# The forward substitution of 32x32 blocks in a hybrid decoder step: from VectorE to GpSimd, with GpSimd's order pinned

## The chip, the cores and the metric

One core of a Trainium2 chip runs the whole program. The metric is the device time of one execution in microseconds (us), from the profiler's clock of the core; the kernel's time is the median of several runs. The engines are named as the profile names them: PE is TensorE (matmuls; PEld its weight loads), DVE is VectorE, ACT is ScalarE, POOL is GpSimd, SP issues the DMAs.

## What is computed

One layer of a hybrid decoder for 2048 new tokens of one sequence and for 8 running sequences with 4 tokens each; the model's width is 1024, all in float32. The normalised rows are multiplied by one wide input weight; a gated convolution and an RWKV-7 time mixing use the product; two output weights, gates, a last weight and a norm close the layer. What matters here is the time mixing, for each of 16 heads:

```python
def step(S, inp):
    r_t, k_t, v_t, d_t, kk_t, a_t = inp
    sa = jnp.einsum('bhvk,bhk->bhv', S, -kk_t)
    S = (S * d_t[:, :, None, :] + sa[..., None] * (kk_t * a_t)[:, :, None, :]
         + v_t[..., None] * k_t[:, :, None, :])
    y = jnp.einsum('bhvk,bhk->bhv', S, r_t)
    return S, y
```

Done in chunks of 64 tokens, the recurrence needs, for each chunk and head, the inverse of a 64x64 unit lower triangular matrix. The kernel inverts its two 32x32 diagonal blocks by forward substitution and joins them by small matmuls.

## The kernel before

**Tiles and stages.** The 2048 tokens are four sets of 512 (the sample tokens go with the last). The main stream of each set is blocks of 24 matmuls: 8 slices of the contraction, each with three products of rounded parts (high by high, low by high, high by low), 128x128 weights by 512 columns, into one of three PSUM banks (`ip`). Each block's result is evicted by ACT and DVE. In set 0 a weight is loaded raw into `wraw`, split into its high and low parts in `whl` (ACT copies the high part, DVE subtracts: the instruction whl<-wraw,whl) and stored; later sets load the parts back.

**The pairs.** Between the main stream's matmuls runs the time mixing of one pair of heads after the other, 8 pairs in each of 4 sets, 32 in all, as `Side` generators: keys (from the projected k, r, v to the scaled AR, BK), solve, merge (the 32x32 inverses joined into Xbd), load (transposes), chain (the recurrence over 8 chunks: pa, UB, pb, SV, S), out (normalisation of the rows Yc and the store). Each has a part of the pair's share of the main stream, from the table CUTS (line 31): its fourth number is where the keys end and the solve begins, its fifth where the solve ends and merge and load begin.

**The solve** (rwkv_solve, line 1177). PE makes the 64x64 scores of 8 chunks and 2 heads, DVE masks them into GM, ACT copies the diagonal blocks to Mc, DVE transposes these into Mi (2.06 us), and then come 31 steps j = 31 to 1 of two instructions on [128, up to 76]: a product into tt and a sum into X. The last step is a 32x32 transposition of X into a tile that bears the name Mi too (in the profile: Mi<-X). Then ACT copies it into Xbd, DVE transposes a part into Mc (Mc<-Xbd), and PE's first merge matmuls read it (pt<-Mc,GM and pt<-Mc,Mo).

**What sets the order.** PE, ACT, DVE and POOL each take their instructions in order. While the program is written, a `Clock` (line 51) places every instruction at an estimated start, from costs per engine and from the ends of what it reads; a Side goes on when its inputs are ready by that clock. For the engines in PLANNED (line 48: DVE and ACT) the order of these starts is pinned at the end (line 1792), except for the kinds in LOOSE, the low parts of the weights among them. POOL's instructions are placed by the same clock, but not pinned. `held` (line 148) keeps the stretches in which DVE, with two inputs that aren't in PSUM, or POOL would hold up the other.

**On POOL before**: the product cv by the gate in the convolution, the two last instructions of out (tmp<-tmp,bv and tmp<-tmp,sz), the power in the norms (mu_), one-column copies between the token shift's `carry` and the tile q (mixed_block, line 838: tmp<-carry when a k, r, v or z block begins, carry<-tmp when it ends; the eviction of a block reads that column), and every second low part of the next set's rows (XL in to_cols, line 754, called from prep, line 765).

Of the kernel before, what the change touches and what calls it, by code (L numbers as in the profile page):

```python
# [11 lines left out]
ALU = mybir.AluOpType  # L12
AX = mybir.AxisListType
PSUM = bass.MemoryType.PSUM
DRAM = bass.MemoryType.DRAM

P = 128
# [10 lines left out]
     "sv": 1.5, "bt": 2.0, "score": 4.0, "inv0": 5.0, "inv": 0.45, "inv1": 4.0, "merge": 2.0,  # L28
     "gk": 1.3, "us": 1.3, "sa": 1.3, "state": 1.3, "samp": 2.0, "gn": 4.0, "out": 2.0}

CUTS = {"most": (0.7, 0.0, 0.0, 0.34, 0.7, 0.95, 0.95), "last": (0.6, 0.3, 0.68, 0.4, 0.7, 0.97, 0.9),
        "end": (0.2,0.03,0.22,0.1,0.25,0.32,0.28)}

TAIL = (0.32,0.52,0.32,0.52,0.65)
# [10 lines left out]
SLACK = 60.0  # L45


PLANNED = ('DVE', 'ACT')


LOOSE = ('prep', 'first', 'late', 'zero', 'low')
# [3 lines left out]
OVERLAP = {"DVE": (83, 13), "ACT": (60, 18)}  # L55


class Clock:
# [72 lines left out]
    def ready(self, aps):  # L131
        return max([e[4] for ap in aps for e in self._hits(ap)], default=0.0)

    def add(self, eng, outs, ins, cost, lag=60.0):
        start = max([self.t["PE"] - PAST if eng in self.busy else self.t[eng]] + [e[4] for ap in ins for e in self._hits(ap) if e[6] != eng] +
                    [e[4] - 26.0 if eng in OVERLAP else e[5] for ap in (*ins, *outs) for e in self._hits(ap) if e[6] == eng] +
                    [self.touched.get((eng, ap.tensor.name), 0.0) for ap in (*ins, *outs)] +
                    [e[5] + 60.0 * (e[7] != eng) for ap in outs for e in self._hits(ap)])
        took = cost
        if eng in OVERLAP:  # L140
            over, drain = OVERLAP[eng]
            p0 = self.boxes(outs[0])[0][0]
            took = cost - over if p0 == 0 else cost + over + 2 * drain
        if eng in self.busy:
            start = self.gap(eng, start, took)
        if eng == "POOL" or eng == "DVE" and sum(ap.space != PSUM for ap in ins) > 1:
            for _ in range(3):
                was = start
                for s, e in sorted(self.held["POOL" if eng == "DVE" else "DVE"]):
                    if s < start + cost and start < e:  # L150
                        start = e
                start = self.gap(eng, start, took)
                if start == was:
                    break
            self.held[eng] = self.held[eng][-60:] + [(start, start + cost)]
        end = start + cost
        for ap in (*ins, *outs):
            self.touched[eng, ap.tensor.name] = start
# [95 lines left out]
class Traced:  # L254
# [5 lines left out]
    def __getattr__(self, op):  # L260
        f = getattr(self.eng, op)

        def call(*a, **k):
            r = f(*a, **k)  # L264
# [6 lines left out]
            at = self.clock.add(self.name, outs, ins, c, late + 60.0)  # L271
            if self.clock.planning and self.clock.kind not in LOOSE and self.name in PLANNED:
                self.clock.begun.setdefault(self.name, []).append((at, r.ins))
            return r
        return call

    def cost(self, op, out, ins, k):
        n = out.free_size()
        if self.name == "PE":
            turned = op == "transpose"  # L280
            lhs, rhs = (ins[0], ins[1]) if turned else (k["lhsT"], k["rhs"])
            part = [next(x for x in (32, 64, 128) if v <= x) for v in (lhs.ap[0][1], lhs.free_size())]
            mode = tuple(part)
            if turned:
                t, late = max(0.85 * n, 30.0), 272.0
            elif rhs.dtype == F32R:
                mode, t, late = (P, P), 8 + 0.4375 * n, 175 + 0.43 * n
            elif mode == (P, P):
                t, late = max(1.667 * n + 3, 216.0), max(382.0 if n >= P else 328.0, 175 + 1.7 * n)
            elif mode == (32, 32):  # L290
                t, late = 30.5 * max(1.0, n / 32), 212.0
            elif mode[1] == 64:
                t, late = (59.6 if mode[0] == 64 else 55.4) * max(1.0, n / 64), 300.0
            elif mode == (64, P):
                t, late = (0.93 * max(n, 64) if n <= P else 0.93 * n), 250 + 1.7 * n
            else:
                t, late = 1.667 * max(n, 32), 300.0
            if mode != self.clock.mode:
                t, late = t + 165, late + 225
                self.clock.mode = mode  # L300
            return t, late - t + SLACK
        if self.name == "DVE":
            per = {"transpose": 1.12 if n <= 256 else 1.86, "tensor_tensor_scan": 2.1, "reciprocal": 6.1}.get(op, 1.05)
            if op == "tensor_reduce":
                n = ins[0].free_size()
            if op == "tensor_scalar" and ins[0].space != PSUM:
                per = 0.587
            one = op == "scalar_tensor_tensor" and isinstance(k["scalar"], bass.AP)
            return 145 + per * n + 58 * one
        if self.name == "ACT":  # L310
            strided = n > 64 and list(ins[0].ap)[-1][0] > 1
            return (155 if ins[0].space == PSUM else 190) + (1.9 if strided else 0.84) * n + 100 * max(0, len(ins) - 1) + 0.0
        if k.get("op") == ALU.pow:
            return 1650.0
        return 120 + 2.3 * n if op == "tensor_tensor" else 120 + 1.0 * n


class Queue:
# [26 lines left out]
def hybrid_kernel(tc, x_prompt, x_sample, state_conv, state_shift, state_rwkv, norm_g, w_in, conv_w,  # L345
# [6 lines left out]
    SP = Queue(nc.sync, clock)  # L352
# [214 lines left out]
    TPS = NT // P  # L567
# [197 lines left out]
    def prep(th, half):  # L765
# [9 lines left out]
        yield "free", xts  # L775
        for q in range(NB // KG):
            for k, (i, xt) in enumerate(zip(mine, xts)):
                to_cols(q, xt, (i - th * TPS) * P, G if k % 2 else V)
                if q == NB // KG - 1 and i < NTL - 1:
                    wraw_p.free(xt)  # L780
                yield 1
# [14 lines left out]
    def late_setup():  # L796

        for i in range(TPS, NTL + 1):
            xt, m = load_x(i)
            yield 1, [xt[0:m]]  # L800
            stat_tile(i, xt, m)
            if i < NTL:
                wraw_p.free(xt)
            yield 1
# [372 lines left out]
    def rwkv_solve(th, p, o):  # L1177
# [7 lines left out]
        for c0 in range(0, NCH + samp, 4):  # L1185
# [6 lines left out]
            k = len(cs)  # L1192
# [22 lines left out]
        for j in range(31, 0, -1):  # L1215
            c0 = j // 4
            tt = sm.tile([P, 80], F32, name="tt")
            tv = tt[:, 0:(8 - c0) * j].rearrange("p (c i) -> p c i", i=j)
            V.tensor_tensor(out=tv, in0=Mi[:, j, 0:j].unsqueeze(1).broadcast_to([P, 8 - c0, j]),
                            in1=X[:, c0:8, j:j + 1].broadcast_to([P, 8 - c0, j]), op=ALU.mult)  # L1220
            V.tensor_tensor(out=X[:, c0:8, 0:j], in0=X[:, c0:8, 0:j], in1=tv, op=ALU.add)
            yield W["inv"]
        Xo = rw.tile([P, 32, 32], F32, name="Mi")[:, 0:8].rearrange("p a (e c) -> p a e c", c=8)
        V.transpose(Xo.rearrange("p a e c -> p (a e c)"), X.rearrange("p a b -> p (a b)"))
        o.update(GM=GM, Xo=Xo, Mo=Mo)
        yield W["inv"]

    def rwkv_merge(th, p, o):

# [330 lines left out]
    def part_of(w, key, j, src, scale=1.0):  # L1560

        hl = qs[turns[0] % 2]
        turns[0] += 1
        yield 1, [src]
        A.activation(out=hl[:, 0], in_=src, func=AF.Copy, scale=scale)
        yield 1, [hl[:, 0]]
        V.scalar_tensor_tensor(out=hl[:, 1], in0=src, scalar=scale, in1=hl[:, 0].bitcast(F32), op0=ALU.mult, op1=ALU.subtract)
        SP.store(units[w][key][j // 2][:, :, j % 2 * 4 * P:(j % 2 + 1) * 4 * P], hl.bitcast(F32))
# [561 lines left out]
```

## Time and profile before

| | |
|---|---|
| median of 3 runs | 3086.65 us (3082.61 to 3088.28) |
| profiled execution | 3081.61 us; its span, first to last instruction, 3079.9 us |
| granted TensorE clock, mean | 0.995 |
| busy: PE, DVE, ACT, POOL | 3004.7, 2140.3, 1338.9, 311.2 us |

A line of instructions reads: line in the code, engine, operation, output<-inputs, partitions x columns, count | busy us, mean ns of one | idle time of the engine ahead of them and who ended it. Nearly all stand under line 264, the helper that records each call, so one goes by the tiles. A line of waits reads: who waited <- for whom: us in total, times, the longest. A line of the timeline reads: start, duration in us, engine, operation, count [idle before <- who ended it]. In a line of windows stand the busy time and the count of PE, PEld, DVE, ACT and POOL. Times in a timeline and a window count from the span's start.

### The profile page before, as it was taken

The page shows a single profiled execution, that of the slowest core. Times are in us where ns is not written, and L with a number is a line of the kernel's source. Part 1 is how long each engine was busy: PE and PEld are TensorE (multiplying, and loading weights), DVE is VectorE, ACT ScalarE, POOL GpSimd, SP SyncE. Part 2 cuts the span into 40 slices and gives each one's busy share as a digit, 9 for nine tenths or more (in the row PEclk, how much of TensorE's full clock was granted, in tenths as well). Part 3 has the DMA queues.
Part 4 walks back from the last instruction along what each step waited for, and adds up shares of the span by engine and source line. Part 5 has one row for each costly group of instructions (what it writes and reads, how often), then busy time and mean ns, then how long its engine had stood idle before and what let it go on. Part 6 is the DMA issues. An engine that isn't in the chain of part 4 may idle for free. (4 is left out here: it accounts for less than half of the span.)

```text
span 3079.9 us, 56086 instructions
## 1 busy us (share of the span) xinstructions
PE 3004.7 (98%) x21418; PEld 2574.5 (84%) x21418; DVE 2140.3 (69%) x5606; ACT 1338.9 (43%) x2691; POOL 311.2 (10%) x520
## 2 busy tenths in 40 slices
PE   7999999999999999899999999999999999999998
PEld 6777877788878788788888889999999999888996
DVE  5777767766777777777766666666676774486575
ACT  5455555544444444444444444444444442224223
POOL 2011111111111110111111111000000000000000
PEclk9999999999999999999999999999999999999999
DMA  7877767656767676766644444444334447987775
GB/s 270 274 241 239 236 210 255 228 193 222 243 222 235 230 241 218 238 225 239 223 169 155 169 152 151 141 148 144 130 129 144 140 156 239 352 332 291 281 261 193
DMA packets 293937, 659.15 MB, mean 214 GB/s; under 512 B 46394, under 2 KB 162227, under 8 KB 242982
## 3 DMA queue, kind: packets, MB, share of 16 engines
q1 hardware_dynamic: 293670, 655.58, 62.4%
q8 instruction: 169, 2.77, 0.3%
q14 instruction: 98, 0.80, 0.1%
HBM read 472.81 MB, written 182.69 MB: 213 GB/s over the span
## 5 line engine op out<-in xcount | busy, mean ns | idle before, releaser
L264 PE MATMUL ip<-XH,whl 128*128 128x512 f32 (+3 forms) x7088 | 1940.8, 353 | 12.4 <-DVE whl L264 6.4
L264 PEld LDWEIGHTS ip<-XH,whl 128*128 128x128 f32 x7088 | 1223.5, 189 | 156.7 <-DVE whl L264 8.8
L264 PE MATMUL ip<-XL,whl 128*128 128x512 f32 (+3 forms) x3544 | 1248.9, 352 | 2.3 <-POOL XL L264 2.3
L264 PEld LDWEIGHTS ip<-XL,whl 128*128 128x128 f32 x3544 | 671.7, 190 | 73.4 <-issue 5.6
L264 DVE TENSOR_TENSOR tt<-Mi,X 128x60 f32<-128x60 f32 (+24 forms) x992 | 216.4, 218 | 28.6
L264 DVE TENSOR_TENSOR X<-X,tt 128x60 f32<-128x60 f32 (+24 forms) x992 | 211.0, 213 | 31.9
L264 DVE SCALAR_TENSOR_TENSOR S<-pb,pe,sp 64x64 f32<-64x64 f32 x512 | 143.4, 280 | 121.5 <-PE pb L264 114.3
L264 ACT COPY SV<-pb 64x128 f32<-64x128 f32 x256 | 66.0, 258 | 320.6 <-PE pb L264 318.3
L264 ACT ACTIVATE sp<-S,pe 128x128 f32<-128x128 f32 x256 | 102.5, 400 | 227.7 <-DVE S L264 226.8
L264 DVE TENSOR_TENSOR UB<-pa,P 64x64 f32<-64x64 f32 x512 | 110.2, 215 | 124.1 <-PE pa L264 109.5
L264 ACT ACTIVATE tmp<-ip,vec 128x512 f32<-128x512 f32 (+2 forms) x174 | 102.9, 593 | 206.5 <-PE ip L264 200.5
L264 PEld LDWEIGHTS pb<-UB,Xbd 128*128 128x128 f32 x512 | 86.6, 189 | 37.2 <-issue 12.8
L264 ACT COPY Xbd<-Mi 32x256 f32<-32x256 f32 x128 | 88.1, 688 | 62.1 <-DVE Mi L264 60.0
L264 ACT ACTIVATE tmp<-ip 128x512 f32<-128x512 f32 (+2 forms) x126 | 63.0, 500 | 115.2 <-PE ip L264 114.7
L264 DVE TENSOR_TENSOR GM<-pt,mask_p 128x512 f32<-128x512 f32 x128 | 82.4, 686 | 43.8 <-PE pt L264 43.7
L264 PE MATMUL pb<-UB,Xbd 128*128 128x128 f32 x512 | 104.4, 285 | 7.5 <-DVE UB L264 6.7
L264 PEld LDWEIGHTS pb<-SV,BKt 128*128 128x128 f32 x512 | 89.8, 189 | 24.4 <-ACT SV L264 10.0
L264 DVE TENSOR_TENSOR whl<-wraw,whl 128x1024 fp32r<-128x1024 f32 x81 | 103.7, 1280 | 8.7 <-ACT whl L264 8.1
L264 PEld LDWEIGHTS pa<-S,AR 128*128 128x128 f32 x512 | 88.4, 189 | 25.4 <-DVE S L264 12.5
L264 PE MATMUL pb<-SV,BKt 128*128 128x128 f32 x512 | 101.2, 279 | 4.8 <-ACT SV L264 4.8
L264 PE MATMUL pa<-S,AR 128*128 128x128 f32 x512 | 102.3, 281 | 2.6 <-DVE S L264 2.4
L264 PE MATMUL acc<-XL,whl 128*128 128x264 f32 (+1 forms) x616 | 97.9, 309 | 0.0
(554 smaller groups left out, 4325.1 us busy)
## 6 DMA issues: line engine op xcount, KB each, us to landing
wraw<-in_w_in_dram SPq DMA_DIRECT2D x81, 512.0 KB
whl<-w_k SPq DMA_DIRECT2D x24, 1024.0 KB
whl<-w_r SPq DMA_DIRECT2D x24, 1024.0 KB
whl<-w_v SPq DMA_DIRECT2D x24, 1024.0 KB
whl<-w_z SPq DMA_DIRECT2D x24, 1024.0 KB
whl<-w_xin SPq DMA_DIRECT2D x24, 1024.0 KB
whl<-w_cg SPq DMA_DIRECT2D x24, 1024.0 KB
whl<-w_zc SPq DMA_DIRECT2D x24, 1024.0 KB
```

Source lines behind the costliest of these rows:

```text
L264: r = f(*a, **k)
```

## The change

- The 62 instructions of the substitution (tt and X) are issued on POOL in place of DVE. The sides yield a wait for X ahead of Mi<-X and for the transposed tile behind it.
- POOL is among the PLANNED engines: the order of its placed starts is pinned.
- The clock's rules: a POOL instruction that follows another of POOL on the same data starts 60 ns after its end; what counts as holding the other engine is a DVE call whose in0 and in1 are both outside PSUM; an instruction that would start inside such a stretch is moved to its end, once. A tensor_tensor of POOL costs 218 + 2.09 n in place of 120 + 2.3 n.
- CUTS: the solve's share begins at 0.30 and ends at 0.68 in the first three sets (before 0.34 and 0.70), begins at 0.33 in the last (before 0.40).
- prep gives all low parts XL of the later sets' rows to DVE (prep_first, set 0, still alternates).
- One more yield for each tile of statistics in late_setup; part_of, which splits the summed weights into high and low, flushes the stores that still wait when one of them reads the tile it is about to write.

```diff
-CUTS = {"most": (0.7, 0.0, 0.0, 0.34, 0.7, 0.95, 0.95), "last": (0.6, 0.3, 0.68, 0.4, 0.7, 0.97, 0.9),
+CUTS = {"most": (0.7, 0.0, 0.0, 0.3, 0.68, 0.95, 0.95), "last": (0.6, 0.3, 0.68, 0.33, 0.7, 0.97, 0.9),
...
-PLANNED = ('DVE', 'ACT')
+PLANNED = ('DVE', 'ACT', 'POOL')
...
-                    [e[4] - 26.0 if eng in OVERLAP else e[5] for ap in (*ins, *outs) for e in self._hits(ap) if e[6] == eng] +
+                    [e[4] - 26.0 if eng in OVERLAP else e[5] + 60.0 * (eng == "POOL") for ap in (*ins, *outs) for e in self._hits(ap) if e[6] == eng] +
...
-        if eng == "POOL" or eng == "DVE" and sum(ap.space != PSUM for ap in ins) > 1:
-            for _ in range(3):
-                was = start
-                for s, e in sorted(self.held["POOL" if eng == "DVE" else "DVE"]):
-                    if s < start + cost and start < e:
-                        start = e
-                start = self.gap(eng, start, took)
-                if start == was:
+        if eng == "POOL" or dual:
+            for s, e in self.held["POOL" if eng == "DVE" else "DVE"]:
+                if s <= start < e:
+                    start = self.gap(eng, e, took)
                     break
...
-        return 120 + 2.3 * n if op == "tensor_tensor" else 120 + 1.0 * n
+        return 218 + 2.09 * n if op == "tensor_tensor" else 120 + 1.0 * n
...
-                to_cols(q, xt, (i - th * TPS) * P, G if k % 2 else V)
+                to_cols(q, xt, (i - th * TPS) * P, V)
...
             xt, m = load_x(i)
+            yield 1
             yield 1, [xt[0:m]]
...
-            V.tensor_tensor(out=tv, in0=Mi[:, j, 0:j].unsqueeze(1).broadcast_to([P, 8 - c0, j]),
+            G.tensor_tensor(out=tv, in0=Mi[:, j, 0:j].unsqueeze(1).broadcast_to([P, 8 - c0, j]),
                             in1=X[:, c0:8, j:j + 1].broadcast_to([P, 8 - c0, j]), op=ALU.mult)
-            V.tensor_tensor(out=X[:, c0:8, 0:j], in0=X[:, c0:8, 0:j], in1=tv, op=ALU.add)
+            G.tensor_tensor(out=X[:, c0:8, 0:j], in0=X[:, c0:8, 0:j], in1=tv, op=ALU.add)
             yield W["inv"]
+        yield 0.0, [X]
...
-        yield W["inv"]
+        yield W["inv"], [Xo]
...
         hl = qs[turns[0] % 2]
+        if any(x[1].tensor.name == hl.tensor.name for x in SP.due):
+            SP.flush(0)
```

How the order moves. POOL, at the solve of pair 21 (set 2, sixth pair of heads), before, from the copy of the decays (pe) to the end of out (bv, sz):

```order
267 L264 COPY pe<-tmp 128x8
268 L264 COPY tmp<-carry 128x1 x2
269 L264 TENSOR_TENSOR cv<-cv,tmp 128x512
270 L264 COPY tmp<-carry 128x1 x2
271 L264 COPY carry<-tmp 128x1
272 L264 TENSOR_TENSOR mu__18020<-nw_18078,mhalf 128x8
273 L264 COPY carry<-tmp 128x1 x2
274 L264 TENSOR_TENSOR tmp<-tmp,bv 128x512
```

The same stretch of POOL in the changed kernel, where each "..." leaves out the further steps of the substitution (36 and 22 instructions):

```order
1646 L260 COPY pe<-tmp 128x8
1647 L260 TENSOR_TENSOR cv<-cv,tmp 128x512
1648 L260 TENSOR_TENSOR tt<-Mi,X 128x31
1649 L260 TENSOR_TENSOR X<-X,tt 128x31
...
1686 L260 COPY tmp<-carry 128x1
1687 L260 TENSOR_TENSOR tt<-Mi,X 128x60
1688 L260 TENSOR_TENSOR X<-X,tt 128x5x12
...
1711 L260 COPY carry<-tmp 128x1
1712 L260 COPY tmp<-carry 128x1
1713 L260 TENSOR_TENSOR mu__17997<-nw_18049,mhalf 128x8
```

The 62 instructions stand between cv and the copies of the carried columns, with one such copy (for the k block) inside; the copies for the r block, and the power of the pair before, stand behind them. Before, the copies for two blocks stood ahead of cv.

DVE at the end of the same solve, before:

```order
2920 L264 TENSOR_TENSOR X<-X,tt 128x8
2921 L264 STREAM_TRANSPOSE Mi<-X 128x256
2922 L264 TENSOR_TENSOR Yc<-pt,Yc 128x512
2923 L264 SCALAR_TENSOR_TENSOR kT<-ip,omu,tmp 128x512
2924 L264 STREAM_TRANSPOSE Mc<-Xbd_207 32x256
```

And in the changed kernel, from the last recurrence step ahead of it:

```order
1567 L260 SCALAR_TENSOR_TENSOR S_439<-pb,pe,sp 64x64 x2
1568 L260 TENSOR_TENSOR Yc<-pt,Yc 128x512
1569 L260 SCALAR_TENSOR_TENSOR kT<-ip,omu,tmp 128x512
1570 L260 TENSOR_REDUCE mu__17997<-Yc 128x8
1571 L260 TENSOR_SCALAR mu__17997<-mu__17997 128x8
1572 L260 TENSOR_TENSOR Yc<-Yc,mu__17997 128x512
1573 L260 TENSOR_REDUCE mu__17997<-tmp 128x8
1574 L260 TENSOR_SCALAR nw_18049<-mu__17997 128x8
1575 L260 SCALAR_TENSOR_TENSOR rT<-ip,omu,tmp 128x512
1576 L260 STREAM_TRANSPOSE Mi<-X 128x256
```

Mi<-X moves from ahead of the eviction of kT to behind that of rT, one block of the main stream later. In PE's order 90 matmuls into ip stood between the last score matmul and the first merge matmul of this pair, and 122 stand there now; the number is 103 to 143 before and 117 to 132 now in sets 0 and 1, without the pairs that prepare the next set.

DVE in the solve of pair 2 (set 0) in the changed kernel, where the weights are split:

```order
216 L260 STREAM_TRANSPOSE Mi<-Mc 128x1024
217 L260 SCALAR_TENSOR_TENSOR S_436<-pb,pe,sp 64x64 x2
218 L260 TENSOR_TENSOR UB_209<-pa,P_2267 64x64 x2
219 L260 TENSOR_TENSOR whl<-wraw,whl 128x1024
220 L260 SCALAR_TENSOR_TENSOR S_436<-pb,pe,sp 64x64 x2
...
225 L260 TENSOR_TENSOR Yc<-Yc,mu__2816 128x512
226 L260 TENSOR_TENSOR whl<-wraw,whl 128x1024
...
230 L260 STREAM_TRANSPOSE Mi<-X 128x256
```

Before, these stood among the 62 instructions of the substitution on the same engine; now they run beside those on POOL.

More of the change, by code (lines that the diff above doesn't have):

```diff
@@ L132, in ready, with add @@
         return max([e[4] for ap in aps for e in self._hits(ap)], default=0.0)
-    def add(self, eng, outs, ins, cost, lag=60.0):
+    def add(self, eng, outs, ins, cost, lag=60.0, dual=False):
         start = max([self.t["PE"] - PAST if eng in self.busy else self.t[eng]] + [e[4] for ap in ins for e in self._hits(ap) if e[6] != eng] +
-                    [e[4] - 26.0 if eng in OVERLAP else e[5] for ap in (*ins, *outs) for e in self._hits(ap) if e[6] == eng] +
+                    [e[4] - 26.0 if eng in OVERLAP else e[5] + 60.0 * (eng == "POOL") for ap in (*ins, *outs) for e in self._hits(ap) if e[6] == eng] +
                     [self.touched.get((eng, ap.tensor.name), 0.0) for ap in (*ins, *outs)] +
@@ L270, in call @@
             c, late = c if isinstance(c, tuple) else (c, 0.0)
-            at = self.clock.add(self.name, outs, ins, c, late + 60.0)
+            dual = self.name == "DVE" and all(isinstance(k.get(x), bass.AP) and k[x].space != PSUM for x in ("in0", "in1"))
+            at = self.clock.add(self.name, outs, ins, c, late + 60.0, dual)
             if self.clock.planning and self.clock.kind not in LOOSE and self.name in PLANNED:
```

## The prediction

> **What bounds the kernel now.** I read the page first: busy shares, and the chain that ended last.
>
> ```profile
> PE 3004.7 (98%) x21418; PEld 2574.5 (84%) x21418; DVE 2140.3 (69%) x5606; ACT 1338.9 (43%) x2691; POOL 311.2 (10%) x520
> PE 31%; DVE 5%; DMA 1%; issue 1%; ACT 1%; POOL 0%; SPq 0%; POOLq 0%; DVEq 0%; ACTq 0%
> ```
>
> TensorE is the bound: it stands still for 3079.9 - 3004.7 = 75 us. VectorE is the second engine, GpSimd nearly idle. Whatever VectorE is spared, the gain can only come out of the waits of PE that end with VectorE. The view of PE's waits lists them:
>
> ```profile
> PE ip L264 <- DVE GM L264: 11.0, 1, 11.0
> PE pb L264 <- DVE UB L264: 6.7, 12, 1.2
> PE ip L264 <- DVE whl L264: 6.4, 4, 2.2
> PE ip L264 <- DVE tmp L264: 6.3, 9, 1.4
> PE pt L264 <- DVE Yc L264: 4.9, 5, 1.7
> PE pt L264 <- DVE Mc L264: 3.4, 7, 0.7
> PE ip L264 <- DVE rT L264: 2.4, 2, 1.5
> PE pa L264 <- DVE S L264: 2.4, 7, 0.6
> PE pt L264 <- DVE tmp L264: 1.8, 3, 0.8
> ```
>
> The first is one wait for the first rows of x, before any solve. Mc is the end of the solve itself. The other seven add up to 30.9 us: the waits that a less loaded VectorE can shorten.
>
> **The change, part by part.**
>
> *The work that leaves VectorE.* The groups:
>
> ```profile
> L264 DVE TENSOR_TENSOR tt<-Mi,X 128x60 f32<-128x60 f32 (+24 forms) x992 | 216.4, 218 | 28.6
> L264 DVE TENSOR_TENSOR X<-X,tt 128x60 f32<-128x60 f32 (+24 forms) x992 | 211.0, 213 | 31.9
> L264 POOL TENSOR_TENSOR XL<-tmp,XH 128x512 fp32r<-128x512 f32 x16 | 20.8, 1299 | 50.1 <-ACT XH L264 50.1
> L264 DVE TENSOR_TENSOR XL<-tmp,XH 128x512 fp32r<-128x512 f32 x16 | 10.9, 683 | 0.6 <-ACT XH L264 0.3
> ```
>
> 427.4 us leave VectorE, 13.4 us for each of the 32 pairs. Of the 16 low parts XL on POOL, the 12 in the later sets come back: 12 x 0.683 = 8.2 us. Of the 30.9 us of waits some is the latency of the awaited instruction itself, so the gain lies between 0 and 30.9; I take two thirds, **-20 us**, since the waits were mostly short ones in an in-order queue in which every second or third instruction was one of the solve.
>
> *The solve on POOL.* In columns: a pair's 31 products cover 1560, the sums as many; 62 instructions, 3120 columns. POOL's large two-input instructions and their spacing:
>
> ```profile
> L264 POOL TENSOR_TENSOR tmp<-tmp,bv 128x512 f32<-128x512 f32 x24 | 30.9, 1289 | 117.3 <-ACT tmp L264 117.3
> L264 POOL TENSOR_TENSOR tmp<-tmp,bv 128x544 f32<-128x544 f32 x8 | 10.8, 1356 | 64.5 <-ACT tmp L264 56.9 <-issue 7.6
> L264 POOL TENSOR_TENSOR f<-f,mhalf 128x1 f32<-128x1 f32 x16 | 12.0, 755 | 456.5 <-DVE f L264 454.6 <-ACT junk L264 1.9
> 207.14 1.29 POOL L264 TENSOR_TENSOR tmp<-tmp,bv 128x512 f32<-128x512 f32 x1 [9.02 <-ACT tmp L264]
> 208.51 1.29 POOL L264 TENSOR_TENSOR tmp<-tmp,sz 128x512 f32<-128x512 f32 x1
> 209.74 0.19 POOL L264 COPY pe<-tmp 128x8 f32<-128x8 f32 x1
> ```
>
> (1356 - 1289) / 32 = 2.09 ns a column, so 1289 - 512 x 2.09 = 219 ns fixed; the dependent second one starts 0.08 us after the first ends; I use 0.07. The solve: 62 x (0.219 + 0.07) + 3120 x 0.00209 = 17.9 + 6.5 = **24.4 us**. No row shows a small two-input add on POOL. Its fixed price lies between that of the eight-column COPY, 0.19, and that of the one-column power, 0.755; I take 0.219, near the lower end, since a power's arithmetic is in the upper row. On VectorE the whole took (pair 21, set 2):
>
> ```profile
> 1688.65 2.06 DVE L264 STREAM_TRANSPOSE Mi<-Mc 128x1024 f32<-128x1024 f32 x1 [0.38 <-ACT Mc L264]
> 1691.67 0.19 DVE L264 TENSOR_TENSOR tt<-Mi,X 128x31 f32<-128x31 f32 x1
> 1708.68 0.17 DVE L264 TENSOR_TENSOR X<-X,tt 128x8 f32<-128x8 f32 x1
> 1708.89 0.45 DVE L264 STREAM_TRANSPOSE Mi<-X 128x256 f32<-128x256 f32 x1
> 1709.97 0.74 DVE L264 SCALAR_TENSOR_TENSOR kT<-ip,omu,tmp 128x512 f32<-128x512 f32 x1
> 1705.90 0.66 PE L264 MATMUL pt<-ident,vT 128*128 128x128 f32 x4
> 1711.37 0.24 PE L264 MATMUL pt<-Mc,GM 32*32 32x32 f32 x2
> 1686.20:1711.40 25.20, 25.20 (x151) 20.48 (x150) 21.81 (x82) 9.39 (x20) 0.24 (x1) 1.00 0.56 196
> 1701.93 0.62 PE L264 MATMUL ip<-XH,whl 128*128 128x512 f32 x2
> 1702.63 0.64 PE L264 MATMUL ip<-XH,whl 128*128 128x512 f32 x2
> ```
>
> That is 17.2 us from the first product to the last sum. So the solve gets 7.2 us longer, and the question is whether PE has that much more to do meanwhile. PE's order is fixed. From the last score matmul (1686.2) to the first merge matmul (1711.4) it worked without a gap through 25.2 us, in which its order has 90 matmuls into ip. In the changed order 122 stand there, and 4 more transposes: at (1702.63 - 1701.93) / 3 = 0.233 each, 25.2 + 32 x 0.233 + 0.7 = **33.3 us**. What must fit: scores to the end of Mi<-Mc, 1690.7 - 1686.2 = 4.5; the solve 24.4; then, as VectorE's order now has it, two one-column copies on POOL and the eviction of rT ahead of Mi<-X, some 0.5 + 0.7; from Mi<-X to the first merge matmul 2.5. Together 32.6: **0.7 us to spare**, if nothing disturbs POOL.
>
> *The two engines in each other's way.* This the trace shows:
>
> ```profile
> 632.16 1.29 POOL L264 TENSOR_TENSOR XL<-tmp,XH 128x512 fp32r<-128x512 f32 x1 [1.82 <-ACT XH L264]
> 632.42 1.08 DVE L264 TENSOR_TENSOR tt<-Mi,X 128x31 f32<-128x31 f32 x1
> 633.54 0.19 DVE L264 TENSOR_TENSOR X<-X,tt 128x31 f32<-128x31 f32 x1
> 146.44 0.74 DVE L264 SCALAR_TENSOR_TENSOR BK<-kT,kkh,tmp 128x512 f32<-128x512 f32 x1
> 146.60 1.74 POOL L264 TENSOR_TENSOR cv<-cv,tmp 128x512 f32<-128x512 f32 x1 [9.84 <-DVE tmp L264]
> L264 DVE TENSOR_TENSOR whl<-wraw,whl 128x1024 fp32r<-128x1024 f32 x81 | 103.7, 1280 | 8.7 <-ACT whl L264 8.1
> ```
>
> A VectorE instruction with both inputs in SBUF, begun under a POOL instruction, takes 1.08 us in place of 0.19 and ends 0.05 after POOL's. The other way round, POOL's cv takes 1.74 in place of 1.29, because BK was running: POOL is let in 0.13 us before BK's end. So one such instruction of 0.68 us, which meets a solve, pushes it back by 0.68 - 0.14 - 0.13 - 0.08 = 0.33 us (0.14 is the part of it that ran ahead of POOL's end, 0.08 the pause that POOL had anyway), and a whl of 1.28 us by 0.93. In VectorE's changed order there stand between Mi<-Mc and Mi<-X, over all pairs, 20 whl and 123 of about 0.68 us (parts of qs and q, Yc, XL): 20 x 0.93 + 123 x 0.33 = 59 us. They are uneven: set 0 has two to four whl in a solve (some 3.0 us a pair), the pairs that prepare the next set eight XL (2.6), the other pairs of sets 1 and most of 2 about six (2.0), the rest one to three. Less 0.7 us of spare where there is that much: 7 x 2.3 + 3 x 1.9 + 10 x 1.3 + 12 x 0.2 = **37 us** that arrive at PE as a wait at the merge. Nothing hides it: PE takes its matmuls in order. Its bounds: 0 and 59.
>
> By the Trainium skill's SBUF — State Buffer (Who interferes with whom) the first to issue keeps the shared ports for its whole instruction. That would be 0.68 and 1.28 us in place of 0.33 and 0.93, some 50 us more in the sum; the two rows above show a smaller loss, and I keep to them.
>
> *The rest.* The extra yield in the statistics and the flush of a pending store in the weight sums move a handful of SP's instructions; weights are fetched up to four blocks ahead, so they cost nothing while that lead lasts, and a block's 24 x 0.233 = 5.6 us if a fetch is late by all of it. The carry copies behind the solve hold back rT's eviction; PE has three banks, so two blocks, 11 us, before it feels that.
>
> **The sum.** -20 + 37 = +17 us on the profiled execution's 3081.6 (span 3079.9), which lies 5.0 under the median of the runs; on the median: 3086.65 + 17 = 3104.
>
> **The rivals.**
>
> *The delays are absorbed (faster).* The spare is larger than in pair 21: sets 0 and 1 have up to 132 matmuls there, and two or three VectorE instructions can fall into POOL's own waits. Then only the gain is left, -20: 3067, between 3056 (all of 30.9) and 3080. For it: 59 us in 32 solves is 1.8 a pair, and 1.1 us more spare would swallow it. Against it: set 0's whl come bunched.
>
> *A small POOL instruction costs more (slower still).* With 0.30 us fixed, 62 x 0.08 = 5 us a pair, 32 x 5 = 160: 3264; with 0.24, 1.3 us a pair, 42: 3146. It decides from 0.7 / 62 = 11 ns on. For it: no row of this size. Against it: the 0.19 of the COPY.
>
> By the GPSIMD Engine Reference of the Trainium skill (Elementwise — side-by-side cycle accounting), POOL needs 1.96 times VectorE's time for a two-input add. On 13.4 us that is an estimate of 26.2 us a pair, 1.8 more than mine, and would put the time near 3162; no run here shows it at this size.
>
> *Nothing happens.* PE is at 98% and gain and delay cancel, or whl and qs slip out of the solves: 3087.
>
> **How the numbers follow.** Forecast 0.38 (its own range 3093 to 3125), absorbed 0.31, dearer POOL 0.13, nothing 0.18. Under 0.2% (6 us) a measurement of this kernel tells nothing. Faster: 0.31 and 0.03 of the last; same: 0.15 of the last; slower: 0.51. The range from 3064 to 3146 leaves out the lower end of the second case and most of the dearer POOL.
>
> **What would show it.** The solve on POOL near 26 us in set 0 and 24.7 in pairs 19 to 22; tt and X of 60 columns near 0.34 us with single ones over 0.7 behind a whl; PE's waits for Mc grown from 3.4 to some 40 us, those for UB, tmp and S shrunk. Wrong: POOL's solves under 23 us, or PE not waiting for Mc at all, or PE waiting for SV or ip's evictions instead.

## The result, and the profile after

The changed kernel takes 3110.42 us (median of 6 runs, 3108.97 to 3113.23), the kernel before 3085.84 on the same chip (6 runs): a ratio of 1.0081, 95% interval 1.0068 to 1.0094. It is 25 us slower. The profiled execution took 3108.97 us with a span of 3107.1, 27.2 longer than before's 3079.9.

The page of the changed kernel, the lines of busy time and of the chain that ended last:

```profile
PE 2999.2 (97%) x21418; PEld 2576.1 (83%) x21418; DVE 1754.3 (56%) x3634; ACT 1341.9 (43%) x2691; POOL 894.9 (29%) x2492
PE 64%; POOL 9%; issue 5%; DVE 5%; ACT 2%; DMA 1%; SPq 0%; POOLq 0%; DVEq 0%; ACTq 0%
```

VectorE was spared 386 us, and GpSimd, at 29% of the span, has appeared in the chain. PE is busy for 5.5 us less, yet idle for 3107.1 - 2999.2 = 107.9 us instead of 75.2. Its waits in the changed kernel:

```profile
PE ip L260 <- DVE whl L260: 35.9, 9, 11.3
PE pt L260 <- DVE Mc L260: 12.9, 9, 4.3
PE ip L260 <- DVE GM L260: 11.2, 1, 11.2
PE ip L260 <- DVE rT L260: 11.1, 4, 4.8
PE ip L260 <- DVE vT L260: 4.7, 1, 4.7
PE pb L260 <- DVE UB L260: 3.1, 7, 1.0
...
PE pa L260 <- DVE S L260: 1.6, 4, 0.6
PE ip L260 <- DVE tmp L260: 1.2, 2, 1.1
```

The short waits that the change was to relieve (UB, S, tmp, Yc) went from 22.1 us to 5.9. Mc, where the prediction put its loss, grew by 9.5 us only. New are the waits of the main stream for whl, rT and vT: 8.8 us before, 51.7 now. For whl PE waits nine times, up to 11.3 us at a time, and the engine named, VectorE, is idle 44% of the span. So one looks at what VectorE itself waits for. The groups of the changed kernel, the eviction of rT:

```profile
L260 DVE SCALAR_TENSOR_TENSOR rT<-ip,omu,tmp 128x256 f32<-128x256 f32 (+3 forms) x59 | 28.3, 509 | 188.4 <-POOL tmp L260 179.5
```

VectorE stands idle 188.4 us ahead of these 59 instructions, 179.5 of them for `tmp` from GpSimd: the one-column copy tmp<-carry. The timeline of the changed kernel in pair 2 (set 0), VectorE, then GpSimd, then PE:

```profile
260.44 1.35 DVE L260 TENSOR_TENSOR whl<-wraw,whl 128x1024 fp32r<-128x1024 f32 x1
...
262.42 0.17 DVE L260 TENSOR_SCALAR nw<-mu__2816 128x8 f32<-128x8 f32 x1
274.04 0.75 DVE L260 SCALAR_TENSOR_TENSOR rT<-ip,omu,tmp 128x512 f32<-128x512 f32 x1 [11.45 <-POOL tmp L260]
274.71 0.43 DVE L260 STREAM_TRANSPOSE Mi<-X 128x256 f32<-128x256 f32 x1
275.07 1.18 DVE L260 TENSOR_TENSOR whl<-wraw,whl 128x1024 fp32r<-128x1024 f32 x1
...
273.56 0.21 POOL L260 TENSOR_TENSOR X<-X,tt 128x8 f32<-128x8 f32 x1
...
273.82 0.18 POOL L260 COPY tmp<-carry 128x1 f32<-128x1 f32 x1
...
269.97 0.39 PE L260 MATMUL ip<-XH,whl 128*128 128x512 f32 x1
276.30 0.80 PE L260 MATMUL ip<-XH,whl 128*128 128x512 f32 x1 [5.94 <-DVE whl L260]
```

Read it from the end. PE stops at 270.36 for a whl, whose split stands on VectorE behind rT. VectorE has stood since 262.6 for rT, which needs one column that GpSimd copies in 0.18 us. The copy stands in GpSimd's pinned order behind all 62 instructions of the solve, the last of which ends at 273.77. A chain of 24 us on one in-order engine has become a lock on a second, and through it on PE.

In this pair the copy's own share is small: Mi<-X stands between rT and the whl and itself needs the last X, so that without the copy the whl would have come only some 0.9 us sooner. In pair 0 nothing but rT stands ahead of the whl, and Mi<-X comes 10 us later:

```profile
118.85 0.75 DVE L260 SCALAR_TENSOR_TENSOR rT<-ip,omu,tmp 128x512 f32<-128x512 f32 x1 [15.70 <-POOL tmp L260]
119.51 2.35 DVE L260 TENSOR_TENSOR whl<-wraw,whl 128x1024 fp32r<-128x1024 f32 x2
```

There PE waits 11.3 us for a whl. The waits in which the copy alone stood ahead of what PE needed (for whl in pairs 0 and 4, for rT and for vT) make up some 33 of the 51.7 us; the two waits of pairs 2 and 3, 12.7 us, had Mi<-X in the way too.

A second cost shows in the granted clock. Windows of the changed kernel across the end of that wait (busy PE, PEld, DVE, ACT, POOL, then the clock):

```profile
273.20:276.60 3.40, 0.30 (x1) 0.30 (x2) 2.44 (x5) 1.39 (x3) 3.19 (x9) 0.75 0.00 0
276.60:280.00 3.40, 3.40 (x9) 2.63 (x9) 3.27 (x8) 1.26 (x2) 0.17 (x2) 0.50 0.92 296
280.00:283.40 3.40, 3.40 (x13) 2.71 (x12) 0.32 (x1) 0.00 (x0) 0.00 (x0) 0.75 0.96 369
283.40:287.00 3.60, 3.60 (x46) 2.71 (x44) 0.75 (x1) 0.69 (x1) 0.18 (x1) 1.00 0.76 255
```

The clock is halved from 274.9 to 281.7: while PE is busy it gets 9 matmuls done in 3.4 us, where 14 fit at 0.233 us each. The whole span can be split in three: the time in which PE is idle; what it loses at half clock, half of the time in which it is busy while the trace's record of the clock shows 0.5; and the rest, PE at work at full speed.

| profiled execution | span | idle | lost at half clock | rest |
|---|---|---|---|---|
| before | 3079.9 | 75.2 | 13.6 | 2991.1 |
| after | 3107.1 | 107.9 | 22.0 | 2977.2 |

So the change gains 14 us of running time, loses 33 us in waits and 8 at half clock.

### The profile page after: what moved, and what is told of

It reads as the page before. It is cut to its first block, busy times and chain, and to the rows that moved or that the text cites. A ratio compares the mean times of both kernels' runs of the same rounds, so it can differ in the third digit from the quotient of the medians.

```text
span 3107.1 us, 56220 instructions
## 1 busy us (share of the span) xinstructions
PE 2999.2 (97%) x21418; PEld 2576.1 (83%) x21418; DVE 1754.3 (56%) x3634; ACT 1341.9 (43%) x2691; POOL 894.9 (29%) x2492
## 3 DMA queue, kind: packets, MB, share of 16 engines
q1 hardware_dynamic: 293670, 655.58, 62.1%
## 4 chain that ended last, share of the span: by engine, by line
PE 64%; POOL 9%; issue 5%; DVE 5%; ACT 2%; DMA 1%; SPq 0%; POOLq 0%; DVEq 0%; ACTq 0%
PE ip L260 39%; PE acc L260 12%; PE pt L260 8%; POOL X L260 4%; POOL tt L260 4%; PE pb L260 3%; PE pa L260 1%; DVE tmp L260 1%; ACT Xbd L260 1%; DVE Mi L260 1%; DVE sq L260 0%; ACT tmp L260 0%; DMA Y<-yr 0%; DVE cv L260 0%; POOL cv L260 0%
## 5 line engine op out<-in xcount | busy, mean ns | idle before, releaser
L260 PE MATMUL ip<-XH,whl 128*128 128x512 f32 (+3 forms) x7088 | 1948.1, 355 | 54.2 <-DVE whl L260 35.9
L260 POOL TENSOR_TENSOR tt<-Mi,X 128x60 f32<-128x60 f32 (+24 forms) x992 | 311.2, 314 | 492.3 <-DVE Mi L260 378.3
L260 POOL TENSOR_TENSOR X<-X,tt 128x60 f32<-128x60 f32 (+24 forms) x992 | 313.1, 316 | 77.5
L260 POOL TENSOR_TENSOR f<-f,mhalf 128x1 f32<-128x1 f32 (+1 forms) x17 | 12.5, 742 | 459.9 <-DVE f L260 458.0
L260 DVE SCALAR_TENSOR_TENSOR rT<-ip,omu,tmp 128x256 f32<-128x256 f32 (+3 forms) x59 | 28.3, 509 | 188.4 <-POOL tmp L260 179.5
L260 POOL TENSOR_TENSOR cv<-cv,tmp 128x512 f32<-128x512 f32 (+1 forms) x32 | 48.2, 1507 | 279.6 <-DVE tmp L260 279.5
L260 POOL COPY pe<-tmp 128x8 f32<-128x8 f32 x40 | 11.1, 280 | 359.5 <-ACT tmp L260 346.8
```

## The experiments

Each kernel was run beside the kernel before (medians of that kernel in the three groups of runs: 3082.0, 3084.0, 3083.6); ratios are to it, with 95% intervals. The two theories: *the held queue* (the carry copies behind the solve stop VectorE) and *the ports* (the solve itself is late at the merge, because VectorE's instructions push it back: the prediction's).

**The carry copies, both on ACT, and both on VectorE.** In the changed kernel; on ACT the same two lines read A.copy:

```diff
-            G.tensor_copy(o["q"][:, 0:1], carry[:, mb:mb + 1])
+            V.tensor_copy(o["q"][:, 0:1], carry[:, mb:mb + 1])
...
-                G.tensor_copy(carry[:, mb:mb + 1], o["q"][:, NT:NT + 1])
+                V.tensor_copy(carry[:, mb:mb + 1], o["q"][:, NT:NT + 1])
```

> The changed kernel with both carry copies of the token shift (tmp<-carry and carry<-tmp) on ACT in place of POOL; the solve stays on POOL. Theory H (held queue): the loss is VectorE standing at the eviction of rT until POOL, behind the 62 instructions, has made its carry copy, with the low parts of whl queued behind it; then PE's waits for whl fall from 35.9 to under 8 us, the gaps of 5 to 11 us in set 0 go, the halved clock that follows them goes too, and the time is 3062 to 3082. Theory P (ports, late solve): the solve is late because VectorE's instructions push POOL back; the copies don't matter, and the time stays at 3100 to 3113.

> The changed kernel with both carry copies on VectorE itself. Theory H: as with ACT, 3062 to 3085, a little dearer because 231 copies of 0.17 us come onto VectorE. Theory P: 3100 to 3113.

On ACT 3058.71 us (0.9924, 0.9908 to 0.9939), on VectorE 3052.25 (0.9902, 0.9886 to 0.9917): 52 and 58 us under the changed kernel, under the kernel before too, and 3 and 10 us below the range that the held queue gave. PE's waits with the copies on VectorE, and VectorE at the place of above (this kernel is some 15 us ahead by then):

```profile
PE pt L260 <- DVE Mc L260: 13.0, 12, 2.4
...
PE pb L260 <- DVE UB L260: 5.3, 12, 1.1
...
PE ip L260 <- DVE whl L260: 3.0, 4, 1.1
```

```profile
255.04 0.75 DVE L260 SCALAR_TENSOR_TENSOR rT<-ip,omu,tmp 128x512 f32<-128x512 f32 x1 [2.09 <-ACT tmp L260]
255.71 0.14 DVE L260 COPY carry<-tmp 128x1 f32<-128x1 f32 x1
255.77 0.14 DVE L260 COPY tmp<-carry 128x1 f32<-128x1 f32 x1
258.54 0.44 DVE L260 STREAM_TRANSPOSE Mi<-X 128x256 f32<-128x256 f32 x1 [2.63 <-POOL X L260]
258.91 1.18 DVE L260 TENSOR_TENSOR whl<-wraw,whl 128x1024 fp32r<-128x1024 f32 x1
```

rT now waits for ACT, as before, and is done before the solve ends. The waits for whl are back at 3.0 us, those for rT and vT are gone from the list; Mc's stay at 13.0. That is the held queue, and the part of the ports is what is left at Mc.

**A control: the copies on ACT in the kernel before.** The same two lines in before.

> Control: the kernel before (solve on VectorE) with the carry copies on ACT. Both theories: nothing stands on POOL that holds the copies there, so 3080 to 3092, no difference that can be measured.

3071.4 us (0.9965, 0.995 to 0.998), 11 us less: the expectation of no change was a miss. But the results of this kernel are wrong (the first output is off by 9%). It lacks the changed kernel's flush in part_of, so that some of the stored parts of the summed weights may have been written over; that this is the reason is argued, not shown. Its instructions are the same in number, and its time is a hint at most that before, too, the copies on GpSimd cost something, behind cv, the powers and out's sums.

**One copy at a time.** The first line alone (tmp<-carry, when a block begins), then the second alone (carry<-tmp, when it ends), on VectorE.

> The changed kernel with only the copy at a block's begin (tmp<-carry, which the eviction reads) on VectorE; carry<-tmp stays on POOL. Theory H: this copy alone is what VectorE stood for, so 3048 to 3066. Theory P: 3100 to 3113.

> The changed kernel with only the copy at a block's end (carry<-tmp, read one set later) on VectorE; tmp<-carry stays on POOL behind the solve. Theory H: the eviction of rT still stands behind the solve, so nothing is won: 3098 to 3113. Theory P: the same.

The first alone gives 3056.61 us (0.9907, 0.9892 to 0.9922), nearly the whole gain; the second 3109.22 (1.008, 1.0065 to 1.0095), nothing. PE's waits and the eviction's group with the second alone:

```profile
PE ip L260 <- DVE whl L260: 37.4, 9, 6.9
```

```profile
L260 DVE SCALAR_TENSOR_TENSOR rT<-ip,omu,tmp 128x256 f32<-128x256 f32 (+3 forms) x59 | 28.3, 508 | 162.8 <-POOL tmp L260 153.9 <-ACT tmp L260 8.7
```

VectorE's idle time ahead of rT, 188.4 us in the changed kernel, is still 162.8. So it is the copy that the eviction reads, as the timeline had it, and not the number of small instructions on GpSimd.

**The solve back on VectorE, with the copies on GpSimd and on VectorE.** In the changed kernel, and in the one with both copies on VectorE:

```diff
-            G.tensor_tensor(out=tv, in0=Mi[:, j, 0:j].unsqueeze(1).broadcast_to([P, 8 - c0, j]),
+            V.tensor_tensor(out=tv, in0=Mi[:, j, 0:j].unsqueeze(1).broadcast_to([P, 8 - c0, j]),
...
-            G.tensor_tensor(out=X[:, c0:8, 0:j], in0=X[:, c0:8, 0:j], in1=tv, op=ALU.add)
+            V.tensor_tensor(out=X[:, c0:8, 0:j], in0=X[:, c0:8, 0:j], in1=tv, op=ALU.add)
```

> The changed kernel with the 62 instructions of the solve back on VectorE; the shares of the solve, the pinning of POOL, the new costs and XL on VectorE stay. What these are worth without the solve: theory H and theory P both say that the loss goes with the solve (3080 to 3095). If the time stays over 3100, the loss is in the shares, the pinning or XL, and both theories fall.

> The changed kernel with the solve and the carry copies both on VectorE: the fourth cell beside the changed kernel (solve and copies on POOL, 3110), the solve alone on VectorE (3070) and the copies alone on VectorE (3052). Theory H: without the solve on POOL the copies have nothing to stand behind, so 3062 to 3074, about as with the solve alone on VectorE; then the solve on POOL by itself is worth 10 to 20 us of gain. Theory P: the solve on POOL is a loss by itself, so this is faster than 3052.

3069.63 us (0.9961, 0.9947 to 0.9975), 10 us below what both theories gave, and 3070.55 (0.9951, 0.9934 to 0.9968), as the held queue has it. The four corners:

| median, us | copies on GpSimd | copies on VectorE |
|---|---|---|
| solve on GpSimd | 3110.4 | 3052.3 |
| solve on VectorE | 3069.6 | 3070.6 |

The place of the copies is worth nothing without the solve beside them, and 58 us with it. The solve on GpSimd is worth -18 us where the copies are free of it, and +41 where they aren't. And all that the change does besides the solve is worth some -13 (3069.6 and 3070.6 against 3082.0 and 3084.0). The corners come from different groups of runs; taken each against the kernel before in its own group, the 58 are 54, the -18 are -16 and the +41 are +37.

One thing these runs leave open. An edit moves more than the copy: the clock places everything anew, and without counting the copies, VectorE's order in the changed kernel and in the one with the copies on VectorE differs in many places, from the 45th instruction on. So the 58 us belong to the copies' place together with the order that the clock makes for it. That the hold itself costs PE tens of microseconds is seen in the changed kernel's waits above; the copies moved within a fixed order were not run.

**The merge later.** With both copies on VectorE, the solve's share of the main stream in the first three sets ends later:

```diff
-CUTS = {"most": (0.7, 0.0, 0.0, 0.3, 0.68, 0.95, 0.95),
+CUTS = {"most": (0.7, 0.0, 0.0, 0.3, 0.72, 0.95, 0.95),
```

> The changed kernel with both carry copies on VectorE (3052.3 us), and in the first three sets the end of the solve's share at 0.72 in place of 0.68: a set takes some 603 us, a pair 75, so PE has 0.04 x 75 = 3.0 us more main stream between the scores and the merge. Ports theory (the solve on GpSimd, pushed back by VectorE's two-input instructions, is late at the merge): PE's waits for Mc, 13.0 us with the copies on VectorE, fall to about 3, and with the halved clock behind the longer of them the time falls by 8 to 12, to 3040 to 3044. If Mc's waits are only what the latency of the transposes costs: Mc stays at 10 or more and the time within 3 us of 3052. Third possibility: the merge, the load and the recurrence now start 3 us later and wait elsewhere (UB, S, Yc up by the same 10): no gain or a loss.

3041.61 us (0.9864, 0.9843 to 0.9886), the fastest of all: 69 under the changed kernel. PE's waits:

```profile
...
PE pb L260 <- DVE UB L260: 5.9, 11, 1.8
PE pt L260 <- DVE Mc L260: 5.1, 7, 1.2
```

Mc falls from 13.0 to 5.1 and UB hardly moves. So the late solve was real: about 10 us by the medians; in the profiled executions 6 less idle time, 4 less at half clock and 2 more in the rest (table below). How much of the lateness is VectorE's pushing and how much the chain's own length on GpSimd, this run doesn't tell.

**A cheaper price, and no pin.** Both with the copies on VectorE. The clock's price of GpSimd's two-input instruction was set to what quiet solves show; in the other kernel GpSimd's order is not pinned:

```diff
-        return 218 + 2.09 * n if op == "tensor_tensor" else 120 + 1.0 * n
+        return 190 + 1.82 * n if op == "tensor_tensor" else 120 + 1.0 * n
```

```diff
-PLANNED = ('DVE', 'ACT', 'POOL')
+PLANNED = ('DVE', 'ACT')
```

> The changed kernel with both carry copies on VectorE (3052.3 us), and the clock's price of a two-input GpSimd instruction set to what the trace shows, 190 + 1.82 n ns in place of 218 + 2.09 n. By the clock each solve then ends 62 x 28 + 3120 x 0.27 ns = 2.6 us earlier and what is behind it on VectorE is placed earlier. If the clock's wrong price is what makes VectorE's order loose (Mi<-X placed behind rT, 0.94 us after X's end): up to 32 x 0.3 = 10 us less where PE waits for Mc; 3042 to 3052. If the solve really ends later than the clock now thinks, because of VectorE's instructions on the ports: instructions placed behind Mi<-X on VectorE wait for it, and the time is 3052 to 3065. I hold it for a change within 5 us.

> The changed kernel with both carry copies on VectorE (3052.3 us), GpSimd's order not pinned (PLANNED as before). VectorE's order is the same row by row; on GpSimd a few small fills come ahead of out's sums. If the pin does nothing once the copies have gone from GpSimd: 3052 within 4 us. If it matters by itself (a rival in which the pinned order rather than the long chain is the harm): 5 us or more away, faster if the pin holds something back, slower if it helps.

Without the pin 3054.1 us (0.9903, 0.9885 to 0.992): the pin matters nothing once the copies are elsewhere. With the copies on GpSimd the pin was not taken out by itself, so what it does there stays open. With the cheaper price 3125.44 (1.0139, 1.0119 to 1.0159): 73 us lost, where I had expected 5 either way, 13 at most. VectorE and PE in that kernel, in the same pair 2, and PE's waits:

```profile
261.52 0.14 DVE L260 COPY tmp<-carry 128x1 f32<-128x1 f32 x1
267.89 0.45 DVE L260 STREAM_TRANSPOSE Mi<-X 128x256 f32<-128x256 f32 x1 [6.23 <-POOL X L260]
268.25 1.18 DVE L260 TENSOR_TENSOR whl<-wraw,whl 128x1024 fp32r<-128x1024 f32 x1
...
265.45 0.39 PE L260 MATMUL ip<-XH,whl 128*128 128x512 f32 x1
269.49 0.50 PE L260 MATMUL ip<-XH,whl 128*128 128x512 f32 x1 [3.65 <-DVE whl L260]
```

```profile
PE pt L260 <- DVE Mc L260: 32.8, 36, 2.1
PE ip L260 <- DVE whl L260: 17.1, 7, 3.9
```

It is the same lock through another door. The clock now believed the solve over 2.6 us sooner than it had, and placed Mi<-X earlier on VectorE; the real solve, which VectorE's own instructions lengthen, was not done; Mi<-X stood, and the whl behind it. The group of Mi<-X with the copies on VectorE, at the old price and at the cheaper one:

```profile
L260 DVE STREAM_TRANSPOSE Mi<-X 128x256 f32<-128x256 f32 x32 | 14.2, 443 | 55.5 <-POOL X L260 52.4 <-POOL tmp L260 3.1
```

```profile
L260 DVE STREAM_TRANSPOSE Mi<-X 128x256 f32<-128x256 f32 x32 | 14.3, 445 | 106.8 <-POOL X L260 103.6 <-POOL tmp L260 3.0
```

VectorE's idle time there doubles. The merge comes sooner in PE's order too: in most pairs of sets 1 and 2, 107 to 110 matmuls into ip stand between the last scores and the merge, where 118 to 124 stood with the old price, and PE's waits for Mc grow from 13.0 to 32.8 us. Of the 81 us between the two profiled spans 45 are idle time and 33 half clock.

**Where the other -13 us come from.** The kernel before, with prep's XL on VectorE and the flush:

```diff
-                to_cols(q, xt, (i - th * TPS) * P, G if k % 2 else V)
+                to_cols(q, xt, (i - th * TPS) * P, V)
...
         hl = qs[turns[0] % 2]
+        if any(x[1].tensor.name == hl.tensor.name for x in SP.due):
+            SP.flush(0)
```

> The kernel before with prep's XL all on VectorE (12 instructions of 0.68 us, which on GpSimd took 1.3 us and held VectorE's solve up, 1.08 in place of 0.19 once) and with part_of's flush. The changed kernel with the solve back on VectorE stood at 3069.6 against 3082 to 3085, so all that the change does besides the solve is worth -13 to -15 us. If that comes from XL: 3068 to 3076. If it comes from the new shares in CUTS, the pin or the clock's rules: 3080 to 3088, no change.

3082.37 us (0.9997, 0.9986 to 1.0009): XL, with the flush, is worth nothing. What remains is the new shares in CUTS, the pin, the clock's rules and the added yields together; they were not tried apart.

**What a wait costs.** In the kernel with both copies on VectorE, six blocks of the main stream were made to wait: VectorE reads the bank of the block ahead, GpSimd raises 32 (or 4) columns to a power, and VectorE writes the result into the new bank, which the block then writes over. Nothing else hangs on it.

```diff
+    STALL = {("cg", 1, 2): 32, ("cg", 1, 4): 32, ("cg", 2, 2): 32, ("cg", 2, 4): 32, ("cg", 1, 6): 4, ("cg", 2, 6): 4}
...
+        V.tensor_scalar(out=a[:, 0:m], in0=lastps[0][:, 0:m], scalar1=0.0, scalar2=2.0, op0=ALU.mult, op1=ALU.add)
+        G.tensor_tensor(out=b[:, 0:m], in0=a[:, 0:m], in1=mhalf[:, 0:1].broadcast_to([P, m]), op=ALU.pow)
+        V.tensor_copy(ps[:, 0:m], b[:, 0:m])
```

> The changed kernel with the carry copies on VectorE (3052), and six waits of TensorE put in on purpose, in sets 1 and 2: before the first matmul of a block, a column range of its bank is written from a POOL power that reads the bank before; four waits with 32 columns (5 to 7 us each), two with 4 columns (1.5 to 2.5 us). The result is not changed by it. Theory T (a wait of TensorE costs twice): 14 to 17 us after each long wait the granted clock falls to 0.5 for 3.4 to 6.8 us, after the short ones it may not; time 3052 + 24 + 4 + 7 to 14 = 3085 to 3096. Rival: the halved clock in the changed kernel is chance; then it stays at the 24 us in all of the kernel without the waits, and the time is 3075 to 3083.

3090.29 us (1.002, 1.0011 to 1.003): 38.0 over the kernel that it was made from. PE's waits of this kind, and the windows from the wait of 1.9 us that begins at 1749.0:

```profile
PE ip L260 <- DVE ip L260: 30.6, 6, 7.7
```

```profile
1749.00:1752.20 3.20, 1.35 (x6) 1.12 (x7) 1.26 (x5) 2.78 (x6) 1.20 (x3) 1.00 0.74 276
1752.20:1755.60 3.40, 3.40 (x12) 2.71 (x11) 1.77 (x5) 0.13 (x1) 0.00 (x0) 0.50 0.15 63
```

Five of the six waits bring the halved clock, 2 to 4 us after their start, for 3.4, 6.8 or 10.2 us; the sixth, of 0.8 us, does not. Where an expectation puts some 14 us between a wait and the halving, it had read the clock's record against the wrong zero: the profile's times count from the first instruction, 11 us after the record's. Hence a part of the halved time lies in the wait itself, where it costs nothing, and these waits cost a quarter more than their length: 38.0 us for 30.6.

The split of the span for the kernels that carry the argument:

| profiled execution | span | idle | lost at half clock | rest |
|---|---|---|---|---|
| after | 3107.1 | 107.9 | 22.0 | 2977.2 |
| copies on VectorE | 3047.6 | 62.1 | 7.6 | 2977.9 |
| only carry<-tmp on VectorE | 3107.4 | 104.3 | 25.3 | 2977.8 |
| solve on VectorE | 3068.3 | 67.3 | 4.3 | 2996.6 |
| copies on VectorE, merge later | 3039.2 | 55.9 | 3.4 | 2979.9 |
| copies on VectorE, cheaper price | 3129.0 | 107.2 | 40.8 | 2981.0 |
| copies on VectorE, six waits | 3088.4 | 91.3 | 17.1 | 2980.0 |

The rest goes with the place of the solve, 2977 to 2981 on GpSimd and 2991 (before) or 2997 on VectorE; idle time and half clock go with the order of the queues.

## Why the prediction was right, and where not

The time, 3110 against 3104, and the sign came out as forecast. The sum that gave them did not: of its two main terms one was four times too large and the other came by a way that the prediction had excluded, and the term that decided the time stood in it as nothing. That the total came within 6 us is luck, as the end of this section shows.

**The relief of VectorE (-20).** Right in size, but by another way. The prediction held that "the gain can only come out of the waits of PE that end with VectorE". The waits for UB, S, tmp and Yc did fall by 16 us in the changed kernel. But between the kernel with the solve on VectorE and the one with the solve on GpSimd and the copies on VectorE, PE's idle time fell by 5 us only; -18.7 us lie in the rest, PE's busy time without what half clock costs. PE's groups of the recurrence in the first and in the second show a third of it:

```profile
L260 PE MATMUL pb<-UB,Xbd 128*128 128x128 f32 x512 | 106.5, 290 | 10.7 <-DVE UB L260 9.6
L260 PE MATMUL pa<-S,AR 128*128 128x128 f32 x512 | 103.6, 284 | 4.5 <-DVE S L260 4.1
```

```profile
L260 PE MATMUL pb<-UB,Xbd 128*128 128x128 f32 x512 | 103.3, 283 | 5.6 <-DVE UB L260 5.3
L260 PE MATMUL pa<-S,AR 128*128 128x128 f32 x512 | 101.4, 280 | 2.7 <-DVE S L260 2.6
```

512 x (7 + 4) ns = 5.6 us are matmuls of the recurrence that last longer where VectorE is late; I take these for waits too short to leave a gap, since a matmul's record (0.39 us) overlaps the next one's start 0.233 us later. Where the other 13 lie I could not show.

**The solve on GpSimd (24.4 us).** Too dear. The first and last of the 62 instructions of pair 21 in the changed kernel:

```profile
1715.76 0.24 POOL L260 TENSOR_TENSOR tt<-Mi,X 128x31 f32<-128x31 f32 x1 [11.62 <-PE pb L260]
...
1738.13 0.21 POOL L260 TENSOR_TENSOR X<-X,tt 128x8 f32<-128x8 f32 x1
```

22.6 us. The prediction had called a solve under 23 us a sign that it was wrong, and on this step it was: the choice between 0.19 and 0.755 us fell on 0.219, and the lower end was right. The rival of a dearer small instruction is out. The products of 60 columns, on GpSimd in the changed kernel and on VectorE before:

```profile
L260 POOL TENSOR_TENSOR tt<-Mi,X 128x60 f32<-128x60 f32 x96 | 32.4, 337 | 6.4
L264 DVE TENSOR_TENSOR tt<-Mi,X 128x60 f32<-128x60 f32 x96 | 21.1, 220 | 2.8
```

That is 1.5 times, disturbances included. The prediction's estimate of 26.2 us by the Trainium skill's GPSIMD Engine Reference (Elementwise — side-by-side cycle accounting) doesn't hold here either: the 1.96 times of the page is measured at 2048 columns.

**The ports (+37 at the merge).** The disturbance itself came as worked out: the solves last 25.1 us on average in sets 0 and 1, 23.6 and 23.8 in sets 2 and 3, against 22.6 undisturbed, together 8 x (2.5 + 2.5 + 1.0 + 1.2) = 58 us, where 59 was the sum. But the solve had been charged 1.8 us too dearly in each of the 32 pairs, as much again in all, so that by the same working the spare was 2.5 us and not 0.7. At PE Mc's waits grew by 9.5 us, not by 37, and the later merge got back 10 us in all. The mechanism was right, the size about a quarter.

**The carry copies (nothing).** This is the step that failed: "The carry copies behind the solve hold back rT's eviction; PE has three banks, so two blocks, 11 us, before it feels that." The copies were seen behind the solve, and rT was seen behind the copies; but only the banks were counted. Behind rT on VectorE there stand also Mi<-X and the low parts whl, and PE needs these for its very next block, whatever banks are free: whl alone stands for 35.9 us of PE's waits. The banks ran out as well: 15.8 us are waits for the evictions of rT and vT, after VectorE had stood for 8 to 15 us, where the prediction allowed 11. The prediction had itself named it as a sign of being wrong that PE waits for ip's evictions. The four corners make the whole 58 us. That the low parts are needed sooner than the banks was to be read in the order already, and the question "what is queued behind the waiting instruction, and who waits for that" had been answered for one follower only.

**The halved clock.** Not in the sum at all, though the mean granted clock of the kernel before is 0.995 and not 1: +8 us of the 27 between the two profiled spans, and 14 of the 59.5 between the changed kernel and the one with its copies on VectorE.

So the sum by what was measured: -13 for the shares, the pin, the rules and the yields together, -18 for the solve on GpSimd (a gain of some 28, of which 10 are lost at the merge), +58 for the held queue: +27, where the medians say +25. This is no check of the parts: they are differences between the same few medians, and the 2 us are the spread between the groups of runs. The prediction's +17 came near by luck: 27 us too much at the merge and 21 too little in gains (20 in place of 28, and the 13 that it left out) stood against the 58 that it put at nothing.

## What to carry to other kernels

Before a long serial chain moves to an idle in-order engine, list every small instruction that stays on that engine, and for each who waits for it and what is queued behind that waiter on its own engine; copies of 0.18 us behind the chain cost 58 us here in the order that the clock made, more than the chain's move could bring. Move such copies to the engine that uses them, then give the chain's consumer room (the merge later by 3 us brought another 10). In a planner, beware of too low a price for a chain: an order that expects a result too early stops an engine that has other work, and 2.6 us too early in each solve cost 73 in all. Whether a price above the measured one helps was not tried.

## What the runs showed of the hardware

A wait of PE cost more than its length: 38.0 us for 30.6 in the run with the six waits. In all the profiled executions, behind the first 30 us, each wait of PE over 2.5 us was followed by a granted clock of 0.5, from 2 to 5 us after the wait's start, for 3.4, 6.8 or 10.2 us. Below 2.5 us the length doesn't tell: a wait of 1.9 us was followed by it in the run with the six waits, one of 2.46 us in the run with only carry<-tmp on VectorE was not, and a few halvings (at 2148 us in the run with the six waits) have no wait of even 0.2 us in the 7 us ahead of them. The halving can outlast the idle time by far, as in this window of the run with the cheaper price, in which PE was busy for 10.04 of 10.20 us:

```profile
1386.00:1396.20 10.20, 10.04 (x82) 8.02 (x83) 2.87 (x7) 5.95 (x12) 2.56 (x2) 0.50 0.47 163
```

The Trainium skill's TensorE: Matmul & The Clock Gate (Part 1: The HAM clock gate) has the clock halved after an idle window of about 3.4 us that runs freely, and released after a busy one. The lengths, multiples of 3.4, agree; that a wait of 1.9 us, shorter than a window, was enough, and that the halving lasted through three windows of work, differ from it, and the measurement decides.

A two-input instruction of n columns on GpSimd takes about 190 + 1.82 n ns in the quiet solves of set 2 (fitted over 8 to 76 columns), less than the 219 + 2.09 n that the prediction drew from the large ones, and dependent ones start about 270 + 1.84 n ns apart.
